# Hybrid trunk kernel: order of q, k and v projections per head pair, place of k's norm and decayed copy, diagonal blocks copied on chip, residual add four blocks later

## The chip, the cores and the metric

The kernel runs on one core of a Trainium2 chip. The core has a matrix engine (TensorE, "PE" in the profile, with its weight loads as "PEld"), a vector engine (VectorE, "DVE"), a scalar engine (ScalarE, "ACT"), a general engine (GpSimd, "POOL") and a queue engine that issues DMA transfers (SyncE, "SP"). Each engine takes its instructions in a fixed order and waits where an input is not there yet. The metric is the device time of one execution in microseconds (us); the kernel before takes 2367.05 us, the median of three runs.

## The reference

One decoder layer on a sequence of 1024 tokens with 1024 channels: a SwiGLU block, a mixer, a second SwiGLU block, each added to the residual x, and a final norm. The mixer projects its normed input once and runs eight heads of a gated delta rule (GDN, head size 128) and sixteen heads of a state-space scan (SSM) beside each other; both outputs together go through `w_out`. The part that matters here is the delta rule, per head:

```python
qkv = silu(causal_dwconv(gdn_qkv, gdn_conv_w))       # 4 taps
q, k, v = split(qkv)
o = gated_delta_rule(q, k, v, g, beta)

# gated_delta_rule, in chunks of 64 tokens:
q = l2_normalize(q) * dk ** -0.5;  k = l2_normalize(k)
decay = exp(gc[l] - gc[s])  for s <= l, else 0        # gc: running sum of g in the chunk
a_low = beta[l] * (k @ k.T) * decay                   # strictly lower
t_inv = inverse(eye + a_low)
u = t_inv @ (v * beta);  w = t_inv @ (k * beta * exp(gc))
qk = (q @ k.T) * decay;  q_dec = q * exp(gc);  k_dec = k * exp(gc[-1] - gc)
for each chunk:                                       # scan
    v_new = u - w @ state
    o = q_dec @ state + qk @ v_new
    state = state * exp(gc[-1]) + k_dec.T @ v_new
```

and after the mixer `x = x + mixed @ w_out`, with the delta rule's and the SSM's outputs side by side in `mixed`.

## The kernel before

All of the layer is one program. Its stages, in order of time: first SwiGLU block (to about 660 us of the profiled execution), SSM heads (to about 980), four pairs of GDN heads (to about 1645), the output projection, which begins while the last pair is still running (to about 1700), the second SwiGLU block and the final norm. Projections are made in float32 quality by three matmuls each (`mm3`, lines 123 to 125: high times high, high times low, low times high).

The work is traced in program order, and a planner sets the order on each engine from estimated times: what is ready earliest goes first, and earlier program text goes ahead where several are ready. A tile with a tag shares that tag's buffers; a new tile waits until an old one in its buffer has been read for the last time.

A head pair `pr` (lines 1107 to 1370) goes through these steps.

- **Projections and convolution** (`conv_silu`, line 776): for each of q, k and v of each head two halves of 512 tokens, 24 matmuls each, into a PSUM bank of tag "pj" (three banks). ACT copies the bank to `pre` (L784) and writes the last tap into the target (L785); DVE adds three taps (L787, three times); ACT applies Silu (L790). The order of the weights is laid down in `w_seq` (lines 631 to 634): q and k of the first head, q and k of the second, v of both, then gate columns z. The weights are split by ACT (L138) and DVE (L139). The targets: q in tag "xst" with two buffers (both held by one pair), k in one tile of two heads that alternates between the pools `g1` and `g3`, v in tag "vt" with one buffer.
- **Decay** (L1138 to L1144): the decay row comes by DMA into `dt`, is masked by POOL (L898) and exponentiated by ACT (L1140, L1143); `qe` is q times its decay. `dt`, `qe`, `u` and `vr` have one buffer each.
- **Products** (L1151 to L1177), two blocks of 128 tokens at a time: k by k and k by q into two PSUM banks of tag "mx" (two banks); the diagonal of k by k gives k's squared norms (`jd`, L1164, into `tk`), from them and beta come `br2` (L1167 to L1169), and DVE forms `u` (L1172) and `dt` (L1175).
- **Transpositions** of q (for its squared norm by ACT, L1208) and of v (L1217), through PE (L1199).
- **Inverse**: the 32-wide diagonal blocks of `u` go through DRAM (L1182, L1225) into a layout in which DVE does forward substitution (L1235, L1237, 31 steps), and come back by DRAM (L1241). The result is loaded twice, into `xd` (L1249) and into the diagonal blocks of `u` (L1250), by 16 DMAs in turn. Two levels of small matmuls (L1258 to L1288) extend the inverse to 64 wide.
- **kd**: k is transposed again by PE into banks of tag "sc", and DVE multiplies by the decay to the end of the chunk (L1297). `kd` has one buffer.
- **Scan** over eight blocks (L1312 to L1356): L1318, L1327, L1332, L1336, L1340 and L1352 depend on each other in this order; L1344 makes the output. Then the output's norm (L1363 to L1368) and its store to `mix_scr` (L1370).

In the output stage, `pair_tile` (L1422) adds four heads' product to a target by L1432. `ms[0]` stands for heads 0 to 3, `ms[1]` for heads 4 to 7. `load_x2` brings x back from DRAM (L1381) into the buffers of `qe`, `dt`, `u` and `vr`.

Of the kernel before, what the change touches and what calls it, by code (L numbers as in the profile page):

```python
# [11 lines left out]
F32 = mybir.dt.float32  # L12
# [9 lines left out]
P = 128  # L22
# [24 lines left out]
def kernel(  # L47
# [1056 lines left out]
    with ExitStack() as cg:  # L1104
        g1 = cg.enter_context(tc.tile_pool(name="gdn1", bufs=1, reuse_waits="tile"))
        g2 = cg.enter_context(tc.tile_pool(name="gdn2", bufs=2, reuse_waits="tile"))
        for pr in range(GH // 2):
# [37 lines left out]


            u = g3.tile([P, 2, NB, P], F32, name="u")
            tk = g2.tile([P, 2, NB], F32, name="tk")
            br2 = g2.tile([P, 2, NB], F32, name="br2")
            beta_p = beta[:, :, hs].rearrange("p b h -> p h b")  # L1150
            for b0 in range(0, NB, 2):  # L1151
# [9 lines left out]
                for i in range(2):  # L1161
                    for c in range(2):
                        jd = g1.tile([P, P], BF16, name="jd")
                        V.scalar_tensor_tensor(out=jd, in0=pgs[i][:, c * 256:c * 256 + P], scalar=1.0, in1=ident,  # L1164
                                               op0=ALU.mult, op1=ALU.mult,
                                               accum_out=tk[:, i, b0 + c:b0 + c + 1])
                V.tensor_scalar(out=tk[:, :, b2], in0=tk[:, :, b2], scalar1=EPS, scalar2=None, op0=ALU.add)  # L1167
                V.reciprocal(out=br2[:, :, b2], in_=tk[:, :, b2])
                V.tensor_tensor(out=br2[:, :, b2], in0=br2[:, :, b2], in1=beta_p[:, :, b2], op=ALU.mult)  # L1169
# [19 lines left out]
            def flat(t):  # L1189
                return t.rearrange("p i b -> p (i b)")  # L1190
# [4 lines left out]
            def turned(src, tag, half):  # L1195
                pt = psum(tag)
                for c in range(4):
                    b = half * 4 + c
                    T.transpose(pt[:, c * P:(c + 1) * P], src[:, b * P:(b + 1) * P], ident)  # L1199
                return pt  # L1200

            for half in range(2):
                pts = [turned(qts[i], "mx", half) for i in range(2)]
# [348 lines left out]
```

## Time and profile before

| what | value |
|---|---|
| runs of the kernel before | 2364.92, 2367.05, 2367.05 us; median 2367.05 |
| profiled execution, its own time | 2362.89 us |
| its span, first to last instruction | 2361.1 us |
| mean granted clock of PE | 0.989 |
| PE busy | 2292.0 us (97%) |
| DVE busy | 1678.7 us (71%) |
| ACT busy | 1069.2 us (45%) |
| POOL busy | 51.5 us (2%) |
| chain that ended last, by engine | PE 85%, DVE 8%, ACT 4%, DMA 1%, issue 1% |
| HBM read, written | 211.55 MB, 67.73 MB |

The busy times are of one profiled execution. Matmuls are pipelined and their ends are modelled, so a matmul of 512 columns shows about 0.39 us and the next one starts about 0.23 us after it. The granted clock says which part of full speed PE had; 1.00 is full speed. Rows of a timeline begin with the start and the length in microseconds, and a bracket at the end holds the idle time of the engine before the instruction and what ended it. Rows of groups hold a count, then the busy time in us and the mean duration in ns, then the idle time before them.

### The profile page before, as it was taken

Reading aid. Unit: us, or ns where it says so; the run is one execution under the profiler, and the core shown is the slowest. Engines: PE = TensorE matmul, PEld = TensorE weight load, DVE = VectorE, ACT = ScalarE, POOL = GpSimd, SP = SyncE. Lnnn points to the kernel's source line nnn. Section 1 sums busy time; section 2 is a strip of 40 time slices with the busy share of each in tenths; the row PEclk is TensorE's granted clock in tenths of the full one; section 3 lists DMA queues with packets and bytes.
Section 4 is the critical chain, followed back from the end, with each engine's and each line's share of the span. In section 5 each row is a group of like instructions: output and inputs, shape, how many; then the busy total and the mean of one; then the engine's idle time right before and its main releaser. Section 6 shows DMA issues by size and latency. Waiting matters only on the chain.

```text
span 2361.1 us, 31003 instructions
## 1 busy us (share of the span) xinstructions
PE 2292.0 (97%) x11766; PEld 1883.5 (80%) x11766; DVE 1678.7 (71%) x2909; ACT 1069.2 (45%) x1928; POOL 51.5 (2%) x101
## 2 busy tenths in 40 slices
PE   7999999999999999999989799999999999999998
PEld 5788888888878888878778688877778888888886
DVE  8967676768765656767574665886688767776687
ACT  7433333343557867843443435412454333334334
POOL 0000000000001100100000000000000000000000
PEclk9999999999999999999989899999999999999999
DMA  3423232664733322223222223343213323229456
GB/s 109 147 90 116 85 116 94 224 231 142 249 110 96 102 72 90 72 58 76 64 50 76 59 77 117 116 153 114 109 64 115 116 86 115 94 99 339 148 157 215
DMA packets 212633, 281.30 MB, mean 119 GB/s; under 512 B 46880, under 2 KB 145244, under 8 KB 211460
## 3 DMA queue, kind: packets, MB, share of 16 engines
q1 hardware_dynamic: 212228, 279.23, 36.5%
q8 instruction: 92, 1.51, 0.3%
q14 instruction: 57, 0.47, 0.1%
q0 software_dynamic: 256, 0.10, 0.0%
HBM read 211.55 MB, written 67.73 MB: 118 GB/s over the span
## 4 chain that ended last, share of the span: by engine, by line
PE 85%; DVE 8%; ACT 4%; DMA 1%; issue 1%; POOL 0%; SPq 0%; DVEq 0%; ACTq 0%
PE ps_pj L123 9%; PE ps_pj L125 9%; PE ps_pj L124 9%; PE ps_pj L334 6%; PE ps_pj L336 6%; PE ps_pj L335 6%; PE ps_mx L334 3%; PE ps_mx L336 3%; PE ps_mx L335 3%; PE ps_pj L555 2%; PE ps_pj L556 2%; PE ps_pj L554 2%; PE ps_oo L335 2%; PE ps_oo L334 2%; PE ps_oo L336 2%
## 5 line engine op out<-in xcount | busy, mean ns | idle before, releaser
L123 PE MATMUL ps_pj<-hhi,whi 128*128 128x512 f32 x832 | 332.3, 399 | 2.7 <-ACT qt L785 2.3
L125 PE MATMUL ps_pj<-hhi,wlo 128*128 128x512 f32 x832 | 333.0, 400 | 0.0
L124 PE MATMUL ps_pj<-hlo,whi 128*128 128x512 f32 x832 | 330.3, 397 | 0.0
L336 PE MATMUL ps_pj<-bh,al 128*128 128x512 f32 x688 | 268.1, 390 | 0.0
L334 PE MATMUL ps_pj<-bh,ah 128*128 128x512 f32 x688 | 267.9, 391 | 0.2 <-ACT m L343 0.2
L335 PE MATMUL ps_pj<-bl,ah 128*128 128x512 f32 x688 | 268.0, 390 | 0.0
L123 PEld LDWEIGHTS ps_pj<-hhi,whi 128*128 128x128 f32 x832 | 157.3, 189 | 33.8 <-ACT qt L785 3.4
L125 PEld LDWEIGHTS ps_pj<-hhi,wlo 128*128 128x128 f32 x832 | 157.3, 189 | 30.7 <-issue 0.7
L124 PEld LDWEIGHTS ps_pj<-hlo,whi 128*128 128x128 f32 x832 | 157.4, 189 | 30.0
L241 ACT CAST ah<-wst 128x512 fp32r<-128x512 f32 x88 | 54.6, 622 | 214.1 <-PE ps_oo L335 130.0
L334 PEld LDWEIGHTS ps_pj<-bh,ah 128*128 128x128 f32 x688 | 129.0, 188 | 27.2 <-ACT m L343 0.6
L335 PEld LDWEIGHTS ps_pj<-bl,ah 128*128 128x128 f32 x688 | 129.2, 188 | 26.7
L336 PEld LDWEIGHTS ps_pj<-bh,al 128*128 128x128 f32 x688 | 129.2, 188 | 26.6
L241 ACT CAST hid<-hraw 128x1024 fp32r<-128x1024 f32 (+1 forms) x84 | 82.3, 981 | 147.2 <-PE ps_oo L556 62.1
L317 DVE TENSOR_TENSOR as<-wst 128x512 f32<-128x512 f32 x220 | 145.0, 683 | 0.4 <-DMA wst<-in_ffn_w_up_dram 0.3
L242 DVE TENSOR_TENSOR al<-as,ah 128x512 fp32r<-128x512 f32 x220 | 140.7, 685 | 5.9 <-ACT ah L241 5.3
L334 PE MATMUL ps_mx<-bh,ah 128*128 128x512 f32 x352 | 138.4, 395 | 4.0 <-ACT m L343 1.3
L335 PE MATMUL ps_mx<-bl,ah 128*128 128x512 f32 x352 | 138.3, 393 | 0.5 <-DVE bl L242 0.5
L336 PE MATMUL ps_mx<-bh,al 128*128 128x512 f32 x352 | 137.6, 391 | 0.3 <-DVE al L242 0.3
L241 ACT CAST ah<-as 128x512 fp32r<-128x512 f32 x220 | 125.0, 618 | 23.2 <-DVE as L317 23.2
L242 DVE TENSOR_TENSOR hid<-hraw,hid 128x1024 fp32r<-128x1024 f32 (+1 forms) x84 | 95.0, 1131 | 33.2 <-ACT hid L241 32.9
L343 ACT COPY m<-ps_pj 128x512 f32<-128x512 f32 x88 | 51.4, 588 | 123.0 <-PE ps_pj L336 120.7
(428 smaller groups left out, 4988.1 us busy)
## 6 DMA issues: line engine op xcount, KB each, us to landing
hraw<-hid_scr SPq DMA_DIRECT2D x70, 512.0 KB, 4.2
hid_scr<-hs SPq DMA_DIRECT2D x110, 256.0 KB, 2.2
wst<-in_ffn_w_down_dram SPq DMA_DIRECT2D x50, 512.0 KB, 4.5
wst<-in_ffn_w_gate_dram SPq DMA_DIRECT2D x22, 1024.0 KB, 5.5
wst<-in_ffn_w_up_dram SPq DMA_DIRECT2D x22, 1024.0 KB, 5.4
wst<-in_w_in_dram SPq DMA_DIRECT2D x16, 1024.0 KB, 5.3
hid_scr<-sg SPq DMA_DIRECT2D x44, 256.0 KB, 2.0
keep<-in_ffn_w_down_dram SPq DMA_DIRECT2D x20, 512.0 KB, 6.2
```

The costliest lines, as they stand in the source:

```text
L123: T.matmul(o, lhsT=wh, rhs=mh, start=first, stop=False)
L124: T.matmul(o, lhsT=wh, rhs=ml, start=False, stop=False)
L125: T.matmul(o, lhsT=wl, rhs=mh, start=False, stop=last)
L241: return (A.copy(out=hi, in_=src), V.tensor_tensor(out=lo, in0=src, in1=hi.bitcast(F32), op=ALU.subtract))
L242: V.tensor_tensor(out=lo, in0=src, in1=hi.bitcast(F32), op=ALU.subtract))
L317: V.tensor_tensor(out=t, in0=v[0], in1=v[1], op=v[2])
L334: T.matmul(bank, lhsT=wh[:, k], rhs=bh[:, k], start=a, stop=False, skip_group_check=True)
L335: T.matmul(bank, lhsT=wh[:, k], rhs=bl[:, k], start=False, stop=False, skip_group_check=True)
L336: T.matmul(bank, lhsT=wl[:, k], rhs=bh[:, k], start=False, stop=z, skip_group_check=True)
L343: A.copy(out=t, in_=bank)
L554: T.matmul(bank, lhsT=hh, rhs=wh, start=first and k == 0, stop=False, skip_group_check=True)
L555: T.matmul(bank, lhsT=hh, rhs=wl, start=False, stop=False, skip_group_check=True)
```

## The change

- k of both heads of a pair is projected and convolved first, then q of both, then v; every weight load is now one DMA of 256 columns.
- k is transposed by PE ahead of the products, into "mx" banks. From the same transposition ACT takes k's squared norms (16 squares a pair) and DVE makes `kd`. `tk`, `br2` are made once per pair for all blocks. The sixteen diagonal products `jd`, the per-block `tk` and `br2`, and the later transposition for `kd` go away.
- The diagonal blocks of `u` are no longer loaded by DMA (L1250) but copied from `xd` by POOL, four copies of 32 partitions.
- In the output stage the second half of heads 0 to 3 is added to `xa`, and the residual x is added four blocks later.

```diff
     for h in range(0, GH, 2):
-        w_seq.extend((COL_Q + i * P, COL_K + i * P) for i in (h, h + 1))
-        w_seq.append((COL_V + h * P, None))
+        w_seq.extend((c + h * P, None) for c in (COL_K, COL_Q, COL_V))
...
-            for i, h in enumerate((h0, h0 + 1)):
-                wa = next_w()
+            wa = next_w()
+            for i in range(2):
+                conv_silu(g1, wa, i, cw_g, 8 + h0 + i, kts[i])
+            wa = next_w()
+            for i in range(2):
                 qts.append(gp.tile([P, L], F32, name="qt", tag="xst", bufs=2))
-                conv_silu(g1, wa, 0, cw_g, h, qts[-1])
-                conv_silu(g1, wa, 1, cw_g, 8 + h, kts[i])
+                conv_silu(g1, wa, i, cw_g, h0 + i, qts[i])
...
+            def turned(src, half):
+                pt = psum("mx")
+                for c in range(4):
+                    b = half * 4 + c
+                    T.transpose(pt[:, c * P:(c + 1) * P], src[:, b * P:(b + 1) * P], ident)
+                return pt
+
+            def squares(pt, ssq, i, half):
+                for c in range(4):
+                    jk = g1.tile([P, P], BF16, name="jk")
+                    A.activation(out=jk, in_=pt[:, c * P:(c + 1) * P], func=AF.Square,
+                                 accum_out=ssq[:, i, half * 4 + c:half * 4 + c + 1])
...
+            kd = g1.tile([P, 2, NB, P], F32, name="kd")
+            for half in range(2):
+                pts = [turned(kts[i], half) for i in range(2)]
+                hb = slice(half * 4, half * 4 + 4)
+                for i in range(2):
+                    squares(pts[i], tk, i, half)
+                    V.tensor_tensor(out=kd[:, i, hb], in0=pts[i].rearrange("p (c l) -> p c l", c=4),
+                                    in1=wend[:, hb, h0 + i:h0 + i + 1].to_broadcast([P, 4, P]), op=ALU.mult)
+            V.tensor_scalar(out=tk, in0=tk, scalar1=EPS, scalar2=None, op0=ALU.add)
+            V.reciprocal(out=br2, in_=tk)
+            V.tensor_tensor(out=br2, in0=br2, in1=beta[:, :, hs].rearrange("p b h -> p h b"), op=ALU.mult)
...
-                for i in range(2):
-                    for c in range(2):
-                        jd = g1.tile([P, P], BF16, name="jd")
-                        V.scalar_tensor_tensor(out=jd, in0=pgs[i][:, c * 256:c * 256 + P], scalar=1.0, in1=ident,
-                                               op0=ALU.mult, op1=ALU.mult,
-                                               accum_out=tk[:, i, b0 + c:b0 + c + 1])
-                V.tensor_scalar(out=tk[:, :, b2], in0=tk[:, :, b2], scalar1=EPS, scalar2=None, op0=ALU.add)
-                V.reciprocal(out=br2[:, :, b2], in_=tk[:, :, b2])
-                V.tensor_tensor(out=br2[:, :, b2], in0=br2[:, :, b2], in1=beta_p[:, :, b2], op=ALU.mult)
...
                     nc.sync.dma_start(out=xd[js, i * NB:(i + 1) * NB], in_=fs_x[i, j].rearrange("b s l -> s b l"))
-                    nc.sync.dma_start(out=u[js, i, :, js], in_=fs_x[i, j].rearrange("b s l -> s b l"))
             V.transpose(out=lv[:, 1], in_=lv[:, 0])
             uc = u.rearrange("p i b l -> p (i b) l")
+            for j in range(4):
+                js = slice(32 * j, 32 * j + 32)
+                G.tensor_copy(uc[js, :, js], xd[js])
...
-            kd = g1.tile([P, 2, NB, P], F32, name="kd")
-            for half in range(2):
-                pts = [turned(kts[i], "sc", half) for i in range(2)]
-                hb = slice(half * 4, half * 4 + 4)
-                for i in range(2):
-                    V.tensor_tensor(out=kd[:, i, hb], in0=pts[i].rearrange("p (c l) -> p c l", c=4),
-                                    in1=wend[:, hb, h0 + i:h0 + i + 1].to_broadcast([P, 4, P]), op=ALU.mult)
...
-    for b in range(NB):
-        V.tensor_tensor(out=xt2[b], in0=xt2[b], in1=xa[b // 2][:, b % 2], op=ALU.add)
-        pair_tile(b, 1, wb, ms[0], xt2[b][:, 512:1024])
+    for b in range(NB + 4):
+        if b < NB:
+            pair_tile(b, 1, wb, ms[0], xa[b // 2][:, b % 2, 512:1024])
+        if b >= 4:
+            V.tensor_tensor(out=xt2[b - 4], in0=xt2[b - 4], in1=xa[b // 2 - 2][:, b % 2], op=ALU.add)
```

More of the change, by code (lines that the diff above doesn't have):

```diff
@@ L1187 @@
             rin = g2.tile([P, 2, NB], F32, name="rin")
[L1189 to L1190 removed]
             rsqrt_into(g2, flat(rin), flat(tk), "rst")
             V.tensor_tensor(out=rin, in0=rin, in1=tk, op=ALU.mult)
[L1195 to L1200, printed above, removed]
             for half in range(2):
[L1203 removed]
+                pts = [turned(qts[i], half) for i in range(2)]
                 for i in range(2):
[L1205 to L1209 removed]
+                    squares(pts[i], ssq, i, half)
             cq = g2.tile([P, 2, NB], F32, name="cq")
@@ L1213 @@
             for half in range(2):
-                pts = [turned(vts[i], "mx", half) for i in range(2)]
+                pts = [turned(vts[i], half) for i in range(2)]
                 hb = slice(half * 4, half * 4 + 4)
```

10 lines of the change are left out of this document (3 added, 7 removed).

## The prediction

> **What bounds the kernel now.** I read the page first, then busy time by stretch, PE's waits, and the order of work in one pair. The page:
>
> ```profile
> span 2361.1 us, 31003 instructions
> PE 2292.0 (97%) x11766; PEld 1883.5 (80%) x11766; DVE 1678.7 (71%) x2909; ACT 1069.2 (45%) x1928; POOL 51.5 (2%) x101
> ```
>
> PE is the engine to watch, and the change adds no matmul and removes none (16 transpositions of k per pair before and after). So a gain can only be time in which PE stands or runs slowly. The next rows are stretches: from:to, length, then busy time and count of PE, PEld, DVE, ACT, POOL, then granted clock, DMA share, GB/s. The first four are the four pairs, each to the end of its scan (last L1344); the last four hold the losses.
>
> ```profile
> 1024.00:1163.90 139.90, 137.69 (x923) 113.86 (x922) 90.46 (x233) 51.54 (x121) 2.23 (x13) 1.00 0.23 61
> 1163.90:1309.70 145.80, 133.27 (x870) 110.08 (x869) 91.42 (x232) 57.52 (x140) 5.18 (x14) 0.94 0.25 66
> 1309.70:1456.50 146.80, 134.30 (x860) 110.63 (x859) 89.97 (x221) 57.65 (x140) 5.15 (x13) 0.93 0.24 68
> 1456.50:1632.00 175.50, 172.87 (x1090) 141.82 (x1090) 128.61 (x300) 66.05 (x147) 4.69 (x3) 1.00 0.37 120
> 1040.00:1060.00 20.00, 17.79 (x103) 14.18 (x102) 14.97 (x53) 9.00 (x37) 0.10 (x1) 1.00 0.30 66
> 1172.00:1204.00 32.00, 19.47 (x95) 16.36 (x95) 21.20 (x76) 12.49 (x49) 1.03 (x2) 0.73 0.26 58
> 1310.00:1352.00 42.00, 29.50 (x135) 24.89 (x133) 28.12 (x90) 19.18 (x62) 3.23 (x3) 0.76 0.31 82
> 1630.00:1672.00 42.00, 33.00 (x145) 25.98 (x145) 38.22 (x60) 14.10 (x25) 0.00 (x0) 0.92 0.66 225
> ```
>
> PE's loss in a stretch is its idle time plus busy time times one minus the clock. Pair 1: 12.5 + 0.27 x 19.5 = 17.8 us. Pair 2: 12.5 + 0.24 x 29.5 = 19.6. Pair 0: 20 - 17.79 = 2.2. Pair 3, over its whole row: 2.6. After the last scan 9.0 + 0.08 x 33 = 11.6. That makes 53.8 us, the **ceiling** of any gain here.
>
> What stops PE in pair 1, in order of time (start, length, engine, line; in brackets the wait and what ended it):
>
> ```profile
> 1171.75 0.39 PE L125 MATMUL ps_pj<-hhi,wlo 128*128 128x512 f32 x1
> 1175.11 0.49 PE L1157 MATMUL ps_mx<-kt 128*128 128x128 f32 x2 [2.97 <-DVE dt L1175]
> 1179.90 0.46 PE L1157 MATMUL ps_mx<-kt 128*128 128x128 f32 x2 [2.66 <-DVE dt L1175]
> 1185.96 0.46 PE L1157 MATMUL ps_mx<-kt 128*128 128x128 f32 x2 [2.66 <-DVE dt L1175]
> 1191.32 1.94 PE L1199 MATMUL ps_mx<-ident,qt 128*128 128x128 f32 x8 [2.66 <-DVE dt L1175]
> 1195.21 0.69 ACT L785 ACTIVATE qt<-ps_pj,cols 128x512 f32<-128x512 f32 x1 [0.41 <-PE ps_mx L1199]
> 1195.95 0.80 PE L123 MATMUL ps_pj<-hhi,whi 128*128 128x512 f32 x1 [0.78 <-ACT qt L785]
> ```
>
> Two things meet. PE waits for DVE block by block, since both "mx" banks are in use. And it has nothing to put between: the next pair's projection begins with q0, whose L785 needs a "qt" buffer that this pair still holds (until L1199 has read it, 1195.21). The three "pj" banks fill up and the projection stands from 1171.75 to 1195.95. Once the fill is gone the clock falls too.
>
> **Filling PE alone gains nothing in the end.** From one scan end to the next runs a chain: dt comes free, exps, products, forward substitution, levels, scan. In pairs 1 and 2 it takes 146 us, with 125 of PE work at full clock (133.27 x 0.94, 134.30 x 0.93). Work pulled forward into the head is missing at the tail. So I cost the chain, with PE's losses as the cap.
>
> **The change part by part.**
>
> *Products.* DVE from the first u of pair 1 (1173.9) to 1192, by group (count | busy us, mean ns | idle before), where 12 "jd" belong to three blocks:
>
> ```profile
> L1172 DVE SCALAR_TENSOR_TENSOR u<-ps_mx,br,dt 128x128 f32<-128x128 f32 x16 | 4.8, 342 | 0.1
> L1164 DVE SCALAR_TENSOR_TENSOR jd<-ps_mx,ident 128x128 bf16<-128x128 f32 x12 | 3.5, 292 | 4.6 <-PE ps_mx L1159 4.4
> L1175 DVE TENSOR_TENSOR dt<-ps_mx,dt 128x256 f32<-128x256 f32 x8 | 3.4, 419 | 0.2
> L1164 DVE DVE_READ_ACCUMULATOR jd<-ps_mx,ident 128x1 f32 x12 | 1.0, 83 | 0.0
> L1168 DVE RECIPROCAL br<-tk 128x4 f32<-128x4 f32 x3 | 0.5, 178 | 0.1
> ```
>
> The three blocks start 1175.11, 1179.90, 1185.96, and the next work at 1191.32: 5.4 us each. The removed ops are (3.5 + 1.0 + about 1.5 for three kinds of small op)/3 = 2.0 us of it. Without them each bank is free after two u and one dt, so PE can refill one while DVE reads the other: (4.8 + 3.4)/4 = 2.05 us per block, about 2.3 with handovers. Saved 3 x 3.1 = 9.3 us a pair. In exchange k's convolution of the next pair now runs in this stretch (terms below).
>
> *k first.* After the products the chain waits for fu, then DVE is still at the next pair's work:
>
> ```profile
> 1194.57 3.56 SPq L1225 DMA_DIRECT2D fu<-fs_u  x8
> fu<-fs_u SPq DMA_DIRECT2D x8, 128.0 KB, 3.2
> L787 DVE SCALAR_TENSOR_TENSOR kt<-pre,cols,kt 128x1024 f32<-128x1024 f32 x3 | 3.8, 1281 | 1.7 <-ACT kt L785 1.7
> L139 DVE TENSOR_TENSOR wlo<-wst,whi 128x1024 fp32r<-128x1024 f32 x2 | 2.4, 1218 | 0.0
> 1213.37 0.21 DVE L1235 TENSOR_TENSOR ft<-fx,fu 128x62 f32<-128x62 f32 x1
> ```
>
> fu lands at about 1198.1 + 3.2 = 1201.3, the substitution starts at 1213.37: 12 us late, behind k0's convolution (3.8, idle 1.7, weights 2.4). With k done in the head these 7.9 us go; what is late next is fu itself. k's buffer alternates between two pools, so it is free when the scan before the last has ended, and four halves of 24 matmuls, 22 us at an estimated 0.23 us each, can stand where PE lost 17.8. The cost: six L787 and two L139, 6 x 1.28 + 2 x 1.22 = 10.1 us of DVE in the head. Best 0 (in gaps), worst all 10.1; I take 5, since DVE waited 4.6 us there. The loads change from halves to whole columns, one DMA fewer for two of the three weights; SP is idle there, so nothing.
>
> *k turned early.* The transpositions and the four kd products (next fence, 686 ns each) move from between levels and scan to the head. kd has one buffer, held by the scan before until its last L1340, so they cannot come much ahead: 4 x 0.69 + three small ops = 3.2 us of DVE, taken as on the path, 0 at best. The 16 new squares on ACT cost 4.4 us by the row of q's squares below, in the time in which ACT waits for dt; 4.4 on the path if that cover is gone. Where they were, DVE did this (pair 1):
>
> ```profile
> 1275.14 0.68 DVE L1288 TENSOR_SCALAR u<-ps_sc 64x512 f32<-64x512 f32 x1 [0.25 <-PE ps_sc L1285]
> 1276.63 2.13 DVE L1297 TENSOR_TENSOR kd<-ps_sc,wend 128x512 f32<-128x512 f32 x3 [0.21 <-PE ps_sc L1199]
> 1278.80 0.42 DVE L1336 TENSOR_TENSOR vn<-ps_sc,br 128x256 f32<-128x256 f32 x1
> L1208 ACT ACTIVATE jk<-ps_mx 128x128 bf16<-128x128 f32 x16 | 4.4, 277 | 17.9 <-PE ps_mx L1199 17.5
> L790 ACT ACT_TABLE_LOAD x1 | 1.3, 1283 | 0.0
> ```
>
> From L1288's end (1275.82) to L1336 there are 3.0 us, three kd among them; the matmul between them alone I estimate at 1.0. Saved 2.0, at best the 2.1 of the three. Silu of k among the Exps of dt may cost two more table loads, 2.6 us of ACT; half of it: 1.3.
>
> *Diagonal by POOL.* SP's issues:
>
> ```profile
> 1249.54 0.48 SPq L1249 DMA_DIRECT2D lv<-fs_x  x1
> 1256.65 0.45 SPq L1249 DMA_DIRECT2D lv<-fs_x  x1
> L1269 POOL MEMSET lv<- 32x512 f32 x4 | 2.1, 517 | 109.2 <-DVE ft L1235 109.2
> L898 POOL TENSOR_SCALAR_AFFINE_SELECT dt<-dt 128x1024 f32<-128x1024 f32 x8 | 13.5, 1692 | 191.6 <-ACT qe L1140 191.4
> L1144 DVE TENSOR_TENSOR qe<-qe,qt x8: 1224/2103/2109, 989.0 to 1475.4; 128x1024 f32<-128x1024 f32 x8
> ```
>
> lv and u loads alternate, 14 issues in 7.11 us or 0.51 each; with eight fewer the last lv load starts 7 x 0.51 after the first, 3.6 us sooner. A POOL copy of 32x512 is not in the trace: between the memset (0.52) and half the select of twice the width (0.85). I take 0.7, as it reads and writes like the select: four copies 2.8 us, hidden behind the 32- and 64-wide levels, since from the last lv issue (1256.65) to L1288, which the second level releases, are 18 us. Without that cover 2.8 of the 3.6 would be lost: bounds 0.8 to 3.6.
>
> The row L1144 shows that POOL can hurt DVE: beside L898 (1169.77 to 1172.92 in pair 1) the product takes 2.10 us instead of 1.22. The Trainium skill, "SBUF — State Buffer", section "Who interferes with whom", says that a VectorE instruction with two SBUF inputs and a GpSimd one that reads SBUF exclude each other for the whole instruction. The trace agrees with it; by that rule the copies block any L787 beside them, 2.8 us x 4 pairs = 11 us less gain if DVE is the path there. In the sum I charge nothing for it, since what DVE does beside the copies is open until the order is known.
>
> *Residual later.* Tiles (b,1) no longer need x back from DRAM. Its waits (SP issues the last two x loads only after vr is stored):
>
> ```profile
> 1640.47 0.79 PE L123 MATMUL ps_pj<-whi,mtt 128*128 128x512 f32 x1 [5.34 <-DVE xt L1432]
> 1650.18 0.80 SPq L1381 DMA_DIRECT2D xt<-x_scr  x2
> 1670.37 0.50 PE L123 MATMUL ps_pj<-whd,mt 128*128 128x512 f32 x1 [3.13 <-DVE xt L1432]
> ```
>
> The 5.34 goes, but the last tiles need pair 3's output, whatever PE did before; what is late next is that output. Taken as 0; bounds -5 and +5, as the eight adds (1.2 us each) may now fall between the last preparations.
>
> *Sum.* Pairs 1 and 2, each: -9.3 + 5 - 7.9 - 2.0 + 3.2 + 1.3 - 3.6 = -13.3. Pair 0 has clock 1.00, and the interval above that is still at full clock, 1175.11 to 1179.90, is 4.8: 3 x (2.3 - 4.8) = -7.5, and -5.6 for kd's old place and SP, k's norm being hidden by projections: -13.1. Pair 3 shares DVE with the output stage, so about half of the products' gain: -5 - 5.6 + 3.2 = -7.4. Together -47, under PE's cap of 53.8. The order on each engine is planned from estimated times, which here missed fu by 12 us; I take off 10 for that. Estimate **-37**. The profiled execution took 2362.89 us (span 2361.1 and 1.8 around it): 2326 after. The median of the runs, 2367.05, lies 4.2 above it: **2330 us**.
>
> **Rivals.**
> *PE-bound.* k's fill removes all losses and the chain keeps up. For it: 22 us of fill against 17.8 and 19.6 us lost. Against: the loss after the last scan hangs on the chain. -50 to -55, 2312 to 2317.
> *The idle time only moves.* The planner keeps the substitution behind convolutions; then only SP's 3.6, kd's 2.0 and part of the products remain, 4 to 6 us a pair, -22: 2345. For it: chain and PE work are two counts, and only the smaller gain shows. Against: removed DVE work is on the path.
> *It doesn't come ahead.* kd's single buffer keeps k's banks occupied, the products wait for them, and gain and loss cancel: 2362 to 2371. Block 0's products, which ran under the scan before (hence only 12 jd in the head), now come behind it.
> *Slower.* One mechanism, DVE's order between scan end and first u: k's convolution (10.1), kd and norm (3.2) all planned ahead of u, a late block 0 (2.05) and two table loads (2.6) give 18.0 us, against 6.0 of removed ops and 5.6 from SP and kd: +6.4 a pair, three pairs, +19, 2386. It decides once the first u starts over 21.6 us after the scan before: the 10.0 of now (1163.9 to 1173.9) and the 11.6 that are taken away elsewhere.
>
> **How the numbers follow.** Forecast (2322 to 2340) 0.46, PE-bound 0.18, idle moves (2341 to 2357) 0.20, nothing 0.07, slower 0.09. Leaving out slower, nothing and the edge of PE-bound gives 2311 to 2357. Within 0.2% (4.7 us) is what a measurement of this kernel cannot tell from no change: faster 0.84, same 0.07, slower 0.09.
>
> **What would show it.** Products blocks 2 to 2.5 us apart; no 24 us hole in the projections of pairs 1 and 2, granted clock 1.0 there; the substitution's start within 5 us of fu's landing; the last lv load 3.5 us after the first; vn 1 us after the last level; scan starts some 133 us apart instead of 146. Wrong if PE's new idle stands in the scans, if the first u of a pair comes over 21 us after the scan before, or if POOL's copies end the wait of the second level.

## The result, and the profile after

The changed kernel takes 2340.86 us (median of 2336.66, 2339.47, 2342.25 and 2344.47), the kernel before 2365.99 beside it: 25 us less, a ratio of 0.9893 with a 95% interval of 0.9875 to 0.9912. The forecast was 2330 with a range of 2311 to 2357, so the time lies inside the range, 11 us above the forecast. Between the two profiled executions the move is 23.4 us (2362.89 to 2339.47) where the sum said 37.

The page of the changed kernel, its first lines:

```profile
span 2337.7 us, 30967 instructions
PE 2286.3 (98%) x11766; PEld 1875.8 (80%) x11766; DVE 1653.2 (71%) x2745; ACT 1082.2 (46%) x2050; POOL 65.2 (3%) x117
```

Busy time by stretch of the changed kernel (columns as in the prediction: from:to, length, PE, PEld, DVE, ACT, POOL, granted clock, DMA share, GB/s). The first row is the end of the SSM stage, the next four are the four pairs, each to the end of its scan, then the stretch after the last scan; the last two are the heads of pairs 1 and 2:

```profile
900.00:1024.00 124.00, 118.03 (x699) 98.44 (x698) 78.80 (x97) 92.06 (x178) 12.49 (x19) 0.97 0.25 81
1024.00:1169.10 145.10, 145.05 (x949) 118.56 (x948) 87.79 (x185) 61.10 (x160) 6.07 (x18) 1.00 0.21 60
1169.10:1306.70 137.60, 136.43 (x907) 111.40 (x906) 84.49 (x192) 64.82 (x176) 8.68 (x18) 1.00 0.25 69
1306.70:1448.90 142.20, 139.80 (x922) 114.60 (x922) 90.43 (x196) 68.70 (x179) 9.79 (x17) 1.00 0.28 84
1448.90:1608.80 159.90, 150.54 (x969) 123.26 (x968) 112.44 (x249) 57.65 (x165) 7.06 (x7) 0.97 0.36 116
1608.80:1667.00 58.20, 57.44 (x265) 46.29 (x264) 50.04 (x86) 20.34 (x35) 0.00 (x0) 1.00 0.54 194
1169.00:1206.00 37.00, 35.85 (x198) 29.75 (x197) 28.25 (x65) 26.39 (x82) 4.32 (x4) 1.00 0.27 70
1306.00:1350.00 44.00, 41.62 (x227) 34.18 (x226) 32.37 (x68) 29.47 (x101) 3.87 (x4) 1.00 0.36 97
```

The losses that the prediction listed are gone: the heads of pairs 1 and 2 lose 1.2 and 2.4 us where it was 17.8 and 19.6, the stretch after the last scan 0.8 where it was 11.6. But two new losses have come: at the end of the SSM stage (124.00 - 118.03 idle, and 3% of 118 in the clock: 9.5 us; the kernel before was full there) and in pair 3 (9.4 idle and 3% of 150.5: 13.9, before 2.6).

Time is read better from the chain. The last `vn` of a pair stands at the end of its scan; `sq` (its last add) at the end of the SSM stage. Each row gives, after the durations, the start of the first and of the last. First the kernel before, then the changed one:

```profile
L1041 DVE TENSOR_TENSOR sq<-sq,xs x6: 1225/1226/1228, 784.7 to 979.0; 128x1024 f32<-128x1024 f32 x6
L1336 DVE TENSOR_TENSOR vn<-ps_sc,br x8: 423/424/425, 1133.1 to 1162.8; 128x256 f32<-128x256 f32 x8
L1336 DVE TENSOR_TENSOR vn<-ps_sc,br x8: 424/424/425, 1278.8 to 1308.5; 128x256 f32<-128x256 f32 x8
L1336 DVE TENSOR_TENSOR vn<-ps_sc,br x8: 423/425/425, 1426.0 to 1455.3; 128x256 f32<-128x256 f32 x8
L1336 DVE TENSOR_TENSOR vn<-ps_sc,br x8: 415/424/425, 1601.5 to 1630.7; 128x256 f32<-128x256 f32 x8
```

```profile
L1040 DVE TENSOR_TENSOR sq<-sq,xs x6: 1224/1225/1226, 787.1 to 982.0; 128x1024 f32<-128x1024 f32 x6
L1334 DVE TENSOR_TENSOR vn<-ps_sc,br x8: 416/425/425, 1138.3 to 1167.9; 128x256 f32<-128x256 f32 x8
L1334 DVE TENSOR_TENSOR vn<-ps_sc,br x8: 425/425/425, 1276.1 to 1305.5; 128x256 f32<-128x256 f32 x8
L1334 DVE TENSOR_TENSOR vn<-ps_sc,br x8: 418/425/425, 1417.2 to 1447.4; 128x256 f32<-128x256 f32 x8
L1334 DVE TENSOR_TENSOR vn<-ps_sc,br x8: 414/424/426, 1578.2 to 1607.6; 128x256 f32<-128x256 f32 x8
```

| us from one scan end to the next | pair 0 (from `sq`) | pair 1 | pair 2 | pair 3 | sum |
|---|---|---|---|---|---|
| before | 183.8 | 145.7 | 146.8 | 175.4 | 651.7 |
| after | 185.9 | 137.6 | 141.9 | 160.2 | 625.6 |
| measured difference | +2.1 | -8.1 | -4.9 | -15.2 | -26.1 |
| predicted | -13.1 | -13.3 | -13.3 | -7.4 | -47 |

From the last `vn` to the end of the span it is 730.4 us before (2361.1 - 1630.7) and 730.1 after. So the whole move arose in these four pairs, and the pattern over the pairs is not the one predicted. `sq` itself starts 3.0 us later in the changed kernel's profiled execution, which is why 26.1 us of the pairs show as 23.4 in the span.

### The profile page after: what moved, and what is told of

Same layout as the page of the kernel before. It is cut to its first block, busy times and chain, and to the rows that moved or that the text cites. A ratio compares the mean times of both kernels' runs of the same rounds, so it can differ in the third digit from the quotient of the medians.

```text
span 2337.7 us, 30967 instructions
## 1 busy us (share of the span) xinstructions
PE 2286.3 (98%) x11766; PEld 1875.8 (80%) x11766; DVE 1653.2 (71%) x2745; ACT 1082.2 (46%) x2050; POOL 65.2 (3%) x117
## 4 chain that ended last, share of the span: by engine, by line
PE 85%; DVE 8%; ACT 4%; DMA 1%; issue 1%; POOL 0%; SPq 0%; DVEq 0%; ACTq 0%; POOLq 0%
PE ps_pj L123 9%; PE ps_pj L125 9%; PE ps_pj L124 9%; PE ps_pj L334 6%; PE ps_pj L335 6%; PE ps_pj L336 6%; PE ps_mx L334 3%; PE ps_mx L336 3%; PE ps_mx L335 3%; PE ps_pj L555 2%; PE ps_pj L556 2%; PE ps_pj L554 2%; PE ps_oo L335 2%; PE ps_oo L334 2%; PE ps_oo L336 2%
## 5 line engine op out<-in xcount | busy, mean ns | idle before, releaser
L334 PEld LDWEIGHTS ps_pj<-bh,ah 128*128 128x128 f32 x688 | 128.9, 188 | 27.3 <-ACT m L343 0.6
L242 DVE TENSOR_TENSOR al<-as,ah 128x512 fp32r<-128x512 f32 x220 | 141.0, 686 | 6.1 <-ACT ah L241 5.6
L343 ACT COPY m<-ps_pj 128x512 f32<-128x512 f32 x88 | 51.4, 588 | 124.0 <-PE ps_pj L336 121.7
```

Source lines behind the costliest of these rows:

```text
L242: V.tensor_tensor(out=lo, in0=src, in1=hi.bitcast(F32), op=ALU.subtract))
L334: T.matmul(bank, lhsT=wh[:, k], rhs=bh[:, k], start=a, stop=False, skip_group_check=True)
L343: A.copy(out=t, in_=bank)
```

## The experiments

In the table all kernels are read in the same way: "pairs" is the time from the last `sq` to the last `vn` of the profiled execution (651.7 in the kernel before), "rest" what is left of the span behind it. The median is set against the kernel before in the same measurement.

| kernel | median, us | against before | ratio, 95% interval | pairs | rest |
|---|---|---|---|---|---|
| changed kernel | 2340.86 | -25.1 | 0.9893 (0.9875 to 0.9912) | 625.6 | 730.1 |
| before + POOL copies | 2343.80 | -22.6 | 0.9907 (0.9892 to 0.9921) | 630.8 | 732.0 |
| before + early norm and kd | 2351.83 | -14.6 | 0.9938 (0.9923 to 0.9953) | 637.5 | 729.4 |
| before + k first | 2376.32 | +9.4 | 1.0033 (1.0023 to 1.0043) | 658.5 | 731.7 |
| changed, DMAs put back | 2364.71 | -2.2 | 0.9991 (0.9974 to 1.0008) | 655.3 | 728.8 |
| changed, DMAs behind lv | 2342.53 | -23.9 | 0.9901 (0.9886 to 0.9916) | 630.2 | 730.2 |
| changed, no k first | 2339.59 | -27.3 | 0.9874 (0.9856 to 0.9892) | 629.5 | 729.1 |
| changed, old residual | 2336.55 | -30.3 | 0.9865 (0.9851 to 0.9880) | 625.8 | 730.5 |
| changed, DVE eviction | 2339.90 | -26.5 | 0.9891 (0.9874 to 0.9907) | 626.2 | 730.5 |
| changed, q first in pair 0 | 2330.19 | -37.6 | 0.9844 (0.9827 to 0.9861) | 615.9 | 730.6 |
| the last three together | 2328.27 | -39.5 | 0.9834 (0.9817 to 0.9850) | 615.8 | 729.4 |
| before + 96 matmuls | 2367.47 | -0.3 | 1.0000 (0.9991 to 1.0009) | 651.2 | 733.1 |
| changed + 96 matmuls | 2356.92 | -10.4 | 0.9958 (0.9941 to 0.9974) | 641.3 | 728.8 |

The rest is 728.8 to 733.1 us in every kernel, whether TensorE idles after the last scan or not. The pairs, 615.8 to 658.5 us, decide nearly alone, and their sum goes with the medians to within some 5 us. Each edit also lets the planner order all engines anew, so a run shows a part together with the order that it got.

### Each part alone, on the kernel before

**The copies.**

```diff
                     nc.sync.dma_start(out=xd[js, i * NB:(i + 1) * NB], in_=fs_x[i, j].rearrange("b s l -> s b l"))
-                    nc.sync.dma_start(out=u[js, i, :, js], in_=fs_x[i, j].rearrange("b s l -> s b l"))
...
+            for j in range(4):
+                js = slice(32 * j, 32 * j + 32)
+                G.tensor_copy(uc[js, :, js], xd[js])
```

> Kernel before with one part of the change: the eight DMAs per pair into the diagonal blocks of u replaced by the four POOL copies; everything else as before. Queue theory: with eight fewer issues the last lv load starts 3.6 us sooner in each pair and the scans follow; the loss after the last scan shrinks by what the chain gains, 4 x 3.6 = 14 us, 2353 us. Theory of sums (taking the copies out of the changed kernel cost 24 us, so putting them in gains as much here): 2343 us. Cover theory: the heads of pairs 1 and 2 still lose 17.8 and 19.6 us, and a shorter chain only brings them sooner: within 5 us of the kernel before.

Measured: -22.6 us. This part alone brings nearly what the whole change brings, with TensorE still idle for 7.0 and 7.3 us in pairs 1 and 2 (12.5 in each before); the cover theory falls. It is also more than the queue theory's 14: by pairs -4.5, -6.8, -9.8 and +0.2 us. The timeline of pair 1 in the kernel before shows the extra:

```profile
1260.00 0.71 DVE L1251 STREAM_TRANSPOSE lv<-lv 128x512 f32<-128x512 f32 x1 [3.29 <-DMA lv<-fs_x]
1263.49 0.21 PE L1258 MATMUL ps_sc<-lv,u 32*32 32x32 f32 x1
```

and in the kernel with the copies:

```profile
1250.26 4.20 POOL L1254 COPY u<-lv 32x512 f32<-32x512 f32 x3 [1.49 <-DMA lv<-fs_x]
1250.80 3.18 DVE L787 SCALAR_TENSOR_TENSOR vt__10403<-pre,cols,vt__10403 128x1024 f32<-128x1024 f32 x2
1253.90 0.70 DVE L1250 STREAM_TRANSPOSE lv<-lv 128x512 f32<-128x512 f32 x1
1254.74 0.21 PE L1260 MATMUL ps_sc<-lv,u 32*32 32x32 f32 x1
```

In the kernel before lv is turned by 1260.71, but the first level starts at 1263.49: its place on PE is behind projections, 2.8 us late. With the copies it starts 0.14 us after the turn. So besides the queue's 3.6 us the planned order on PE fits better; this is read from pair 1 alone, and why the planner puts it so was not tried. All copies of the four pairs, in the changed kernel:

```profile
L1259 POOL COPY u<-lv 32x512 f32<-32x512 f32 x16 | 12.7, 794 | 15.5 <-DMA lv<-fs_x 14.8
```

The copies do meet DVE: two L787 beside them take 3.18 us; in the kernel before the same two took 2.60. The Trainium skill, "SBUF — State Buffer", section "Who interferes with whom", says that a VectorE instruction with two SBUF inputs and a GpSimd one that reads SBUF exclude each other; the trace agrees, with 0.6 us on DVE here.

**Early norm and kd.** The changed kernel with the projections' order, the DMAs and the residual of before.

> Kernel before with one part of the change: k's transposition, norm and kd ahead of the products, without the diagonal products; old order of projections, diagonal of u by DMA, old residual. Chain theory: products -9.3, kd's old place -2.0, head +3.2 and +1.3, some -7 a pair in three pairs: -21 against the kernel before, 2346 us, and the blocks of products 2 to 3 us apart. Theory of sums: this kernel is the changed one without k first (which cost nothing to take out) and without the copies (which cost 24 us), so 2364 us, no gain.

Measured: -14.6 us, between the two. The four blocks of products of pair 1 now take 9.3 us, 2.3 each, as predicted. What the sum had wrong lies ahead of them. Groups on DVE between scan end and last product of pair 1 (1159.5 to 1189):

```profile
L1171 DVE TENSOR_TENSOR kd<-ps_mx,wend 128x512 f32<-128x512 f32 x4 | 2.8, 689 | 4.6 <-ACT jk L1159 4.6
```

kd waits 4.6 us for ACT's squares. The changed kernel shows why (ACT, then DVE, pair 1):

```profile
1173.29 1.28 ACT L1141 ACT_TABLE_LOAD   x1
1177.89 4.80 ACT L1144 ACTIVATE dt<-dt,ngc 128x128 f32<-128x128 f32 x16 [1.04 <-POOL dt L897]
1182.59 0.25 ACT L1160 ACTIVATE jk<-ps_mx 128x128 bf16<-128x128 f32 x1
1183.70 0.69 DVE L1172 TENSOR_TENSOR kd<-ps_mx,wend 128x512 f32<-128x512 f32 x1 [4.77 <-ACT jk L1160]
1190.01 0.87 DVE L1192 SCALAR_TENSOR_TENSOR u<-ps_mx,br,dt 128x128 f32<-128x128 f32 x3
```

Six of the sixteen squares stand ahead of the Exps of dt in ACT's order; the other ten come behind them, and with them `tk`, `br2` and the first u.

**k first.** `w_seq` and the convolutions of the changed kernel, all else as before.

> Kernel before with one part of the change: k of both heads projected and convolved first, whole columns per weight; products with their diagonals, kd, the DMAs and the residual stay as before. Two theories stand against each other. Chain theory (the prediction's): a chain from scan end to scan end sets each pair, filling TensorE gains nothing by itself; here it saves the 7.9 us of the substitution's late start and pays 5 us of k's convolution in the head, some 3 us a pair in three pairs: -9 against the kernel before, 2357 us. Work theory (from the changed kernel's trace): TensorE's lost time is what counts. The losses of 17.8 and 19.6 us in the heads of pairs 1 and 2 are filled, and the loss at the end of the SSM stage, 9.5 us in the changed kernel, appears here too, since it comes from k going first: -37 + 10 = -27 against the kernel before, about 2339 us, with granted clock 1.0 in the heads of pairs 1 and 2.

Measured: +9.4 us, where both theories expected a gain. Busy time in the heads of pairs 1 and 2 of this kernel, then in the scans of pairs 1 and 3:

```profile
1184.00:1216.00 32.00, 28.78 (x158) 23.76 (x156) 26.27 (x78) 18.62 (x60) 2.73 (x3) 1.00 0.37 101
1328.00:1370.00 42.00, 35.71 (x191) 28.86 (x190) 34.68 (x88) 24.42 (x68) 3.42 (x4) 1.00 0.32 82
1289.00:1321.00 32.00, 25.29 (x169) 20.65 (x168) 14.62 (x39) 9.55 (x38) 0.00 (x0) 1.00 0.01 1
1610.00:1640.00 30.00, 21.88 (x147) 17.77 (x146) 11.31 (x34) 9.02 (x39) 0.00 (x0) 1.00 0.07 20
```

The heads lose 3.2 and 6.3 us in place of 17.8 and 19.6, at full clock. The work that fills them is missing later: TensorE now stands 6.7 and 8.1 us in the scans, waiting for DVE from step to step. The four pairs take 195.6, 144.6, 147.9 and 170.4 us: pairs 1 and 2 are as before, pair 3 is 5 us shorter, and pair 0 is 12 longer (the version with q first, below, shows where). The whole-column loads came with this part and were not tried alone.

### Taking parts out of the changed kernel

**DMAs back in turn.**

```diff
+                    nc.sync.dma_start(out=u[js, i, :, js], in_=fs_x[i, j].rearrange("b s l -> s b l"))
...
-                G.tensor_copy(uc[js, :, js], xd[js])
```

> Changed kernel with the eight DMAs per pair for the diagonal blocks of u put back in turn with those for xd, and the four POOL copies taken out; all else stays. Chain theory: the last lv load is issued 3.6 us later in each of four pairs, +14 against the changed kernel, 2355 us. Work theory: the chain now has slack, TensorE works on in the time: within 4 us of the changed kernel, 2337 to 2345 us.

Measured: 2364.71, 23 us slower than the changed kernel (-2.2 and -25.1 against the kernel before beside each), and no longer told apart from the kernel before. The work theory falls; the chain theory has the sign and is short by 9. Part of this excess is clock. Stretches of pair 1's levels in this kernel:

```profile
1271.60:1276.20 4.60, 3.33 (x162) 3.00 (x161) 1.38 (x2) 2.80 (x5) 0.00 (x0) 0.80 0.92 306
1276.20:1291.00 14.80, 14.80 (x85) 11.99 (x82) 2.18 (x4) 2.24 (x4) 0.00 (x0) 0.50 0.05 18
```

and in the changed kernel:

```profile
1263.30:1274.60 11.30, 11.30 (x241) 8.95 (x240) 2.74 (x4) 2.59 (x5) 0.00 (x0) 1.00 0.20 67
```

With the DMAs the 32-wide levels run with no projection between them, and TensorE is granted half its clock for the next 14.8 us. From the turned lv (1270.0) to the first `vn` it takes 20.9 us here and 15.1 in the changed kernel.

**The same DMAs, behind the lv loads.**

```diff
+            for i in range(2):
+                for j in range(4):
+                    js = slice(32 * j, 32 * j + 32)
+                    nc.sync.dma_start(out=u[js, i, :, js], in_=fs_x[i, j].rearrange("b s l -> s b l"))
...
-                G.tensor_copy(uc[js, :, js], xd[js])
```

> Changed kernel with the eight DMAs per pair for the diagonal blocks of u in place of the POOL copies, but issued behind all eight lv loads instead of in turn with them. Queue theory (what costs is that each lv load waits behind an issue for u): the lv loads are as early as in the changed kernel, and u's diagonal is needed only by the second level and the scan: within 5 us of the changed kernel, 2336 to 2346 us. Traffic theory (what costs is eight more small DMAs at all, or what SP issues behind them): as with the DMAs in turn, 2358 to 2365 us.

Measured: 2342.53, as the changed kernel. Not eight DMAs cost the time, nor does POOL save it: it is their place between the lv loads. In the changed kernel's queue the eight loads run through in 3.92 us (before: 1249.54 to 1257.10, 7.56 us):

```profile
1255.40 3.92 SPq L1254 DMA_DIRECT2D lv<-fs_x  x8
```

and with the DMAs behind them in 3.93, the eight for u after them:

```profile
1258.36 3.93 SPq L1254 DMA_DIRECT2D lv<-fs_x  x8
1262.33 4.15 SPq L1260 DMA_DIRECT2D u<-fs_x  x8
```

**The order of projections.** The changed kernel with q and k by heads again.

> Changed kernel with the order of projections put back (q and k of the first head, q and k of the second, then v); k's early transposition, norm and kd, the copies on POOL and the late residual stay. Chain theory: the removed work on the chain is still gone (products -9.3, kd's old place -2.0, SP -3.6, head +3.2 a pair), only the fill and the earlier substitution are missing: about -11 in three pairs, -33 against the kernel before, 2333 us, faster than the changed kernel or equal to it. Work theory: nothing fills the heads, since the next pair's projection begins with q, whose buffers are held; the heads of pairs 1 and 2 lose again at least half of 17.8 and 19.6 us, while the 9.5 us at the end of the SSM stage go: slower than the changed kernel by 5 to 15 us, 2346 to 2356 us, with TensorE idle in the heads.

Measured: 2339.59; against the changed kernel no difference that these intervals can tell. The chain theory had this right (equal, though not its 2333). The pairs show that k first is not without effect, but pays back what it takes:

```profile
L1333 DVE TENSOR_TENSOR vn<-ps_sc,br x8: 424/425/425, 1124.2 to 1152.7; 128x256 f32<-128x256 f32 x8
L1333 DVE TENSOR_TENSOR vn<-ps_sc,br x8: 416/425/426, 1262.1 to 1291.7; 128x256 f32<-128x256 f32 x8
L1333 DVE TENSOR_TENSOR vn<-ps_sc,br x8: 416/425/425, 1396.3 to 1425.8; 128x256 f32<-128x256 f32 x8
L1333 DVE TENSOR_TENSOR vn<-ps_sc,br x8: 414/424/426, 1579.0 to 1609.4; 128x256 f32<-128x256 f32 x8
```

Pairs 1 to 3 take 139.0, 134.1 and 183.6 us here, with k first 137.6, 141.9 and 160.2; pair 0 takes 172.8 (its last `sq` starts at 979.9), with k first 185.9. k first gains 23 us in pair 3 and loses 13 in pair 0 and 8 in pair 2. Most of pair 3's gain lies between scan end and first u: 41.1 us here (1425.8 to 1466.9), 22.3 in the changed kernel (1447.4 to 1469.7). ACT's table loads in this stretch (1427 to 1467):

```profile
L1128 ACT ACT_TABLE_LOAD x3 | 3.8, 1283 | 0.1
L1143 ACT ACT_TABLE_LOAD x3 | 3.8, 1283 | 0.1
L1140 ACT ACT_TABLE_LOAD x1 | 1.3, 1283 | 0.0
```

Without k first the Silus of z (L1128) are still to come when pair 3's dt arrives, and ACT changes tables seven times; the changed kernel does so once between 1449 and 1470. TensorE's work moves along with these Silus. Pair 3's stretch without k first holds 1063 matmuls, with k first 969 (the row from 1448.90 above):

```profile
1427.00:1610.50 183.50, 177.56 (x1063) 145.54 (x1063) 118.50 (x253) 74.13 (x181) 7.06 (x7) 0.94 0.36 116
```

Four halves of z, 96 matmuls or some 22 us at 0.23 us each, are projected in pair 3 here, and none with k first. So what pair 3 gains is to a good part work that is done earlier, and pairs 0 and 2 pay for it. How much of the 23 us is ACT's order and how much this work, no run separates.

**The residual.** The old loop over tiles put back.

> Changed kernel with the residual added as before (x into xt2 ahead of the second half of heads 0 to 3). Chain theory: what is late at the end is pair 3's output, so nothing changes: within 5 us of the changed kernel. Work theory: the loss after the last scan, 11.6 us before and under 1 us in the changed kernel, was TensorE waiting for x, and comes back: +11, 2352 us.

Measured: 2336.55. Its interval overlaps that of the changed kernel, and the pairs (625.8 against 625.6) and the rest (730.5 against 730.1) are the same. TensorE's wait for xt is 1.2 us in it. The late residual changes nothing once pair 3's output comes sooner.

### Is TensorE the bound?

All kernels but the two with added matmuls run the same 11766 matmuls, so a shorter span must show in the end as less idle time of TensorE or a fuller clock. Span less PE busy is 69.1 us in the kernel before, 51.4 in the changed one, 78.6 with k first alone and 44.7 in the version with q first below. The question is whether filling a hole shortens the span or only opens another.

**Eviction by DVE.**

```diff
-            A.mul(out=o, in_=p, mul=r)
+            V.tensor_scalar(out=o, in0=p, scalar1=r, scalar2=None, op0=ALU.mult)
```

> Changed kernel with one line more: the first group's products of the output stage (the multiplication by r into xa) are evicted by DVE instead of ACT. In the changed kernel TensorE stands 7.3 us in pair 3's head for such an eviction, which lies on ACT behind the Exps of dt, and runs at a granted clock of 0.74 afterwards, 10.4 us lost in all. Work theory: TensorE's losses are what counts, this one goes: -10 against the changed kernel, 2331 us. Chain theory: pair 3's chain from scan to scan is what ends the GDN stage, the work is done later anyway: within 4 us of the changed kernel.

Measured: 2339.90, no change. PE's waits in the changed kernel:

```profile
PE ps_pj L123 <- ACT xa L1407: 7.3, 1, 7.3
PE ps_mx L1044 <- DVE sq L1040: 6.1, 2, 5.8
```

and with the eviction on DVE:

```profile
PE ps_pj L123 <- DVE xt L1430: 4.7, 1, 4.7
```

The 7.3 us are gone; a wait of 4.7 stands after the last scan instead. The same work, done earlier, is missing later: the work theory falls here.

**96 matmuls more in each kernel.**

```diff
+        if twice_v[0]:
+            for k in range(NK):
+                mm3(p, hi[:, k, cs], lo[:, k, cs], hsl(hhi, k, ts), hsl(hlo, k, ts), k == 0, k == NK - 1)
+            twice_v[0] = False
         return p
```

> Kernel before with 24 matmuls of 128x512 more per pair: the first half of v's projection is computed twice into the same bank, the second pass overwrites the first; nothing else is added. 24 x 0.23 = 5.5 us of TensorE work a pair, 22 us in four pairs. Work theory (TensorE busy 97%, so what is added there is added to the time): +20 to +22, 2387 us. Chain theory (the chain from scan to scan sets the end, TensorE's idle time only lies where the work is missing): the heads and the stretch after the last scan have 40 to 50 us of lost time, which the added work cannot fill in place but which moves: under +10, 2367 to 2376 us.

> Changed kernel with the same 24 matmuls of 128x512 more per pair (first half of v's projection computed twice, the second pass overwrites the first), 22 us of TensorE work in four pairs; in the kernel before they cost nothing. Room theory: the changed kernel has used up the idle time that took them in there, it loses under 1 us after the last scan and 2 us in pairs 1 and 2, so at least half of the 22 us now shows: +11 to +22, 2352 to 2363 us. Chain theory without such a limit: the chain from scan to scan still sets the end alone: within 5 us of the changed kernel, 2336 to 2346 us.

Measured: the median of the kernel before does not move (2367.47, interval of the ratio 0.9991 to 1.0009); the changed kernel becomes 15 us slower (-25.1 to -10.4 against the kernel before). The page of the kernel before with them says:

```profile
span 2365.7 us, 31220 instructions
PE 2313.2 (98%) x11862; PEld 1900.6 (80%) x11862; DVE 1677.0 (71%) x2909; ACT 1076.3 (45%) x1932; POOL 52.1 (2%) x101
```

Span less PE busy falls from 69.1 to 52.5 us in the kernel before, and from 51.4 to 45.5 in the changed kernel (span 2350.6, PE 2305.1): the first took 17 us of the work into its holes, the second 6. A busy share of 97% or 98% does not say that. The Trainium skill, "Perfetto Trace Analysis", section "Identifying the Most-Contended Engine", warns that matmul busy time does not tell how far TensorE is from its limit, and names MFU (the arithmetic of the matmuls as a share of the peak) and the share of weight loads instead. The runs agree with the warning; the weight loads stand at 80% in both kernels without the addition, so they don't tell the two apart either. What the room was is seen only by adding work.

Read as in the table of pairs, neither result is the same in all pairs. The changed kernel with the addition takes 189.8, 136.7, 134.6 and 180.2 us (185.9, 137.6, 141.9 and 160.2 without it), the kernel before 186.3, 141.3, 141.0 and 182.6 (183.8, 145.7, 146.8 and 175.4). So its zero is a sum: 10 us less in pairs 1 and 2, 10 more in pairs 0 and 3. In the changed kernel the loss is pair 3's, into which z's projections now fall (five of their sixteen halves, none without the addition). Whether it is TensorE's lack of room or this new order that costs the 15 us, these two runs do not separate. ACT in pair 3's head of the changed kernel with the added work (1442 to 1487):

```profile
L1136 ACT ACT_TABLE_LOAD x4 | 5.1, 1283 | 0.3 <-DMA z_scr<-zc 0.3
L1151 ACT ACT_TABLE_LOAD x4 | 5.1, 1283 | 0.1
```

### A better version

**q first in the first pair.**

```diff
-        w_seq.extend((c + h * P, None) for c in (COL_K, COL_Q, COL_V))
+        w_seq.extend((c + h * P, None) for c in ((COL_Q, COL_K, COL_V) if h == 0 else (COL_K, COL_Q, COL_V)))
```

with the two convolutions in the same order.

> Changed kernel with q projected ahead of k in the first pair only; the other pairs keep k first. In the changed kernel TensorE loses about 8 us at the end of the SSM stage (idle 5.78 us ahead of L1044, then a low clock), because ACT writes the first half of k only at 981.65, when the SSM stage's last squares are done. Buffer theory: k's tile shares memory with tiles of the SSM stage, q's doesn't, so with q first the 8 us go, pair 0's chain and the last scan's end come 5 to 8 us sooner: 2333 to 2336 us. Rival: ACT's order around the last squares makes the stall whatever is projected: no change, 2341 us.

Measured: 2330.19, 11 us below the changed kernel, more than the 5 to 8 expected; 10 of them are pair 0's, which takes 175.9 us instead of 185.9. In the changed kernel ACT copies k's first two banks to `pre` at 958.00 and 972.19, but writes k itself only behind the last squares of the SSM stage:

```profile
979.56 2.19 ACT L1039 ACTIVATE xs<-zt 128x1024 f32<-128x1024 f32 x2 [6.80 <-DVE zt L1033]
981.65 1.25 ACT L784 ACTIVATE kt<-ps_pj,cols 128x512 f32<-128x512 f32 x2
```

With q first the wait at L1044 is gone, TensorE is full from 900 to 1024, and the last `vn` starts at 1595.0 instead of 1607.6. That it is k's memory which the SSM stage still holds is argued from these rows; another place for the tile was not tried.

**This, the DVE eviction and the old residual together.**

> Changed kernel with q ahead of k in the first pair, the first group of the output stage evicted by DVE, and the residual added as before. If gains of chain and of TensorE's work add where both are short: -6 for q first, -4 for the residual, and the eviction's 10 us, which alone brought 1, now count as far as the chain is ahead of the work: -10 to -16 against the changed kernel, 2325 to 2331 us. If the last scan's end alone decides (span = end of the last scan + 730 us in all ten kernels so far): -9, 2332 us, with the last scan ending near 1600 us.

Measured: 2328.27. The pairs are as with q first alone (615.8), and so is the time, within the intervals; the gains don't add, the end of the last scan decides. It is 39.5 us below the kernel before (ratio 0.9834) and 13 below the changed one.

## Why the prediction was right and wrong

- **"Filling PE alone gains nothing in the end": right, the main point.** k first alone filled the heads and was slower, the DVE eviction moved 7.3 us of idle time to another place, and 22 us of added matmuls left the kernel before at its time. It is not a rule for every hole: the one at the end of the SSM stage, closed by q first in pair 0, gave 11 us. What the prediction did not see is that TensorE is nearly full in the changed kernel's pairs 0 to 2 (0.1, 1.2 and 2.4 us idle), so that little of the same kind is left there.
- **Diagonal by POOL, -3.6 a pair: right mechanism, size short.** Alone it gave 22.6 us in place of 14, all of it in pairs 0 to 2. Missing was the first level's place on PE, 2.8 us behind its input in pair 1. The copies took 0.79 us each in the mean where 0.7 was taken, and none ended a wait of the second level. That a change of order on SP would have done as well was not seen.
- **Products 5.4 to 2.3 us a block: right** (2.3 without k's convolution between them, 13.5 us for four in pair 1 of the changed kernel, where it lies between).
- **"16 new squares ... in the time in which ACT waits for dt": wrong, the step that failed.** Ten of pair 1's sixteen squares come after the Exps on ACT, and DVE's `kd` waits 4.6 to 4.8 us for them, on the path to the first u; "4.4 on the path if that cover is gone" was the right bound. The first u of pair 1 starts 21 us after the scan (1169.1 to 1190.0), in pair 2 26 us, which is over the 21 that the prediction named as a sign of being wrong. The text held that above 21.6 us the kernel would be slower. It was not: from first u to scan end the chain fell by 19 us in pair 1, from 135.8 to 116.7, not by the 11.6 that this point of decision was worked out with. Why the squares stand there is in part open: the second half of k can only be turned when `kd` has read a bank, but the second bank of the first half was ready before the Exps (its first square runs at 1172.31), and ACT's planned order put most of its squares behind them.
- **k first, -2.9 a pair: wrong.** In the changed kernel its value is nil, made of +13 in pair 0, +8 in pair 2 and -23 in pair 3; alone it cost 9.4 us. Pair 0 was said to have k's norm "hidden by projections"; k's buffer there was not looked at. Pair 3's gain by early z was not seen at all. The substitution came 6.5 us after fu landed (9.4 in pair 2), not within 5.
- **kd's old place -2.0: right**, `vn` follows the last level by 0.7 us.
- **Residual 0: right.**
- **The 10 us taken off for the planner** did not stand for one cause; it covered the squares and pair 0's late start together, and so -37 was nearer than -47. That the time lies inside the range is in part luck. The three parts, each alone on the kernel before, were expected to give -14, -21 and -9 by the terms of the sum and gave -22.6, -14.6 and +9.4, together -27.8, close to the -25.1 of the whole: the copies gave more than they were credited with, and so covered part of what k first and the squares cost. The range held; the forecast's sum over the pairs did not.
- **The rivals.** TensorE as the bound: its time was not reached; for the changed kernel the added matmuls speak for it, without proving it. "The idle time only moves": the measured 2340.86 lies on the border between the forecast's own stretch (to 2340) and this rival's (from 2341), and it has half the mechanism: the planner did keep the substitution late, but the products and the loads were worth more than it allowed.

## What to carry to other kernels

Test for a bound by adding work to the engine, not by its busy share, and look where the added time falls, since the work can also shift the order of the rest; the time from one fixed point of the chain to the next tells more than the idle time of the busiest engine. In a queue that issues in order, look first at which load the chain waits for and put it ahead of its neighbours; here the order of sixteen issues a pair was worth 22 us (2364.71 to 2342.53), more than the 14.6 of the early norm and `kd`. An instruction moved ahead is only hidden if the buffers that it reads and writes are free and its engine's earlier work is done: check both for each pair of a loop, the first and the last too.

## What the runs showed of the hardware that was not expected

- TensorE lost its clock without a long idle time: two waits of 0.78 and 0.48 us between 32x32 matmuls (together the 1.27 that the row 1271.60 to 1276.20 of the kernel with the DMAs put back lacks), and then 0.50 of the clock for 14.8 us in which it was busy throughout. With projections of 512 columns between the same levels it kept 1.00. The Trainium skill, "TensorE: Matmul & The Clock Gate", section "What's actually happening", gives about 3.4 us of idle time for the fall and about as long under load for the return; neither fits this stretch.
- The part of the program that sets the time repeats to within a microsecond: the pairs take 625.6, 625.8 and 626.2 us in three kernels that have them in the same order, while the SSM stage's end lies anywhere from 978.6 to 983.9. The clock goes with it: in seven of the fourteen profiled executions TensorE has half its clock for 3.4 us shortly after 844 us (846.40 to 849.70 in the changed kernel: 0.50), while it is busy, and there the stage ends at 980.5 or later; the other seven show 1.00 in that stretch and end it by 979.9. The instructions up to there are the same in all of them. A difference of a few microseconds between two executions can be that and nothing else.
